# Seven products instead of eight in the down projection of a SwiGLU layer, on eight cores

## The chip, the cores and the metric

One Trainium2 chip, one launch on its 8 cores, 4 on each die. Each core computes a quarter of one sequence (2048 of the 16384 tokens) through the whole two-layer network; the cores do not exchange data. The metric is the device time of the slowest core in microseconds (us). A kernel has a fast state and, in some executions, a slow one, in which the cores of one die show a lower granted clock.

Names used below: PE is the matmul engine, DVE the vector engine, ACT the scalar engine, POOL the GpSimd engine. PSUM is the memory that PE writes its products to; the kernel uses eight banks of it (`ps0` to `ps7`), and a bank stays taken until its result has been read. A slab is a piece of a weight matrix that one transfer brings in. A "call" is one pass of the feed-forward layer (FFN) over half of a core's tokens, two tiles of 512. There are four: call 1 and 2 in layer 0 (first and second half of the tokens), call 3 and 4 in layer 1. "First-half calls" are 1 and 3, "second-half calls" 2 and 4. After call 2 the mixer and the attention of layer 1 follow; after call 4 the final norm and the store.

## The reference, cut to what matters

```python
D_MODEL, BATCH, SEQ, DEPTH = 1024, 2, 8192, 2
D_FF = 2816                                  # 22 chunks of 128

def swiglu(n, w_gate, w_up, w_down):
    return (jax.nn.silu(n @ w_gate) * (n @ w_up)) @ w_down

# in each of the two layers:
#   h = h + mixer(rms_norm(h))               (convolution in layer 0, gated MLP in layer 1)
#   h = h + cross_attention(rms_norm(h), memory)
#   h = h + swiglu(rms_norm(h, g_ffn[i]), ffn_w_gate[i], ffn_w_up[i], ffn_w_down[i])
# return rms_norm(h, g_final)
```

## The kernel before

The code is cut and shortened. Gate and up already use seven products for eight (Winograd's form of Strassen's scheme). A unit covers two hidden chunks of 128 for two token tiles: the weights are a 2 x 2 of blocks (2 chunks by 2 halves of the 1024 inputs), the tokens a 2 x 2 too (2 tiles by 2 halves). Each "p" below is a group of four matmuls of 512 columns; `g` is 0 for gate and 1 for up.

```python
FPARTS = (12, 10)                     # hidden chunks in each part
AHEAD = {"pe": 6, "act": 32, "dve": 32, "pool": 1, "sp": 1}     # window of the list scheduler
SWITCH = 4.0                          # its penalty for an ACT function of another table

# ffn_pair(): raw = weight block, sm = weight sum (sw), B11.. = tokens nT, T1, T2, T4 = token differences tw
def p1(g):                            # Z = A11 B11, copied to W
    mm(Z[g], raw(g, 0, 0), B11, False)
    act(self.ps[W[g]], self.ps[Z[g]])
def p5(g): mm(R[g], sm(g, 0), T1, False)
def p6(g):
    mm(Z[g], sm(g, 1), T2, True)      # onto Z
    act(V[g], self.ps[Z[g]])          # snapshot of the running sum
def p2(g): mm(W[g], raw(g, 0, 1), B21, True)    # + silu (g=0), product into hid (g=1)
def p7(g):
    mm(Z[g], raw(g, 1, 0), T3, True)  # snapshot Y, then DVE: Y = R + Y ...
def p4(g): mm(Z[g], raw(g, 1, 1), T4, True)
def p3(g): mm(R[g], sm(g, 2), B22, True)        # DVE: V = R + V ...
steps = ((p1,0),(p1,1),(p5,0),(p5,1),(p6,0),(p6,1),(p2,0),(p7,0),(p7,1),(p2,1),(p4,0),(p4,1),(p3,0),(p3,1))

# ffn(l, h): each part is gate and up, then a plain down projection of that part
for part, nf in enumerate(FPARTS):
    for i in range(nf // 2):
        ...                                        # weight sums one unit ahead, on DVE
        self.ffn_pair(*slabs[i], tts, i, npair + i, later)
    if part == 1 and h == 0:
        self.token_sums((2, 3))                    # differences of the next half's tokens
    if final and h == 1 and part == 1:
        self.last_down(l, tts, nf)                 # last tile in two halves of 256 columns
        continue
    for m in range(KC):
        w = self.wc(f"fd{part}", l, m)
        for ti, tt in enumerate(tts):
            ...   # linear(): nf matmuls; DVE: hT += ps; in the last part also the square for the next norm

# schedule(): of the ready instructions in an engine's window the one with the smallest
# due time (worked back from the end) goes first
o = min((o for o in go if o.ready <= t + self.SLIP),
        key=lambda o: (o.due + (self.SWITCH if o.table not in (None, table) else 0.0), o.n))
```

The softmax here doesn't subtract the row's maximum and nothing guards it: scores larger than these inputs give would overflow.

## Time and profile before

Median 1645.21 us of 6 runs (1641.37 to 1799.38). The stages of the program, read off PE's timeline as the distance between the first matmuls of consecutive stages, agree to 0.2 us in the FFN on all cores (but for call 1 on core 3, 210.8 us) and vary by several us in the rest:

| stage before | us |
|---|---|
| start to the first FFN call | 446 to 454 |
| call 1 / 2 / 3 | 209.7 / 210.3 / 209.7 |
| mixer and attention of layer 1, between call 2 and 3 | 332 to 337.5 |
| call 4 up to the mark | 197.8 |
| tail: from the mark to the end | 23.1 |

The mark is PE's first down matmul after the two 512-wide matmuls that sum the first tile's squares for the final norm (1619.3 us on the profiled core). PE's timeline shows rows of 256-wide matmuls from there on, and the expectations below call it the first half-wide matmul; but the first 256-wide matmul comes 4.8 us earlier (1614.5), inside a merged row. The prediction counts its tail, 27.9 us, from that one.

### The profile page before, as it was taken

To read this page: it belongs to the slowest core of one execution; us is meant where nothing else is said; L and a number is where in the kernel's file an instruction comes from. 1 tells how busy PE (TensorE), PEld (TensorE's weight loads), DVE (VectorE), ACT (ScalarE), POOL (GpSimd) and SP (SyncE) were. 2 spreads that over 40 slices of the span, in tenths; PEclk is the share of its full clock that TensorE was granted. 3 is DMA by queue.
4 is the path that set the end of the run, shared out by engine and by line. 5 is a ranking of instruction groups with operands and counts; after the bars stand their busy time and mean duration, and the time that the engine had idled before them with its cause. 6 is when DMAs were issued, how large, how long until landed. Compare 5 with 4: busy or idle time off the path is not lost.

```text
span 1642.4 us, 24105 instructions; the slowest of 8 cores (1629.0 to 1642.4 us)
## 1 busy us (share of the span) xinstructions
PE 1588.2 (97%) x7920; PEld 762.9 (46%) x7920; DVE 1025.9 (62%) x1662; ACT 712.3 (43%) x1176; POOL 71.3 (4%) x149
## 2 busy tenths in 40 slices
PE   5899899999999999999999999999999999999998
PEld 2344484444444444444443455544444444444445
DVE  3638856656787367683654864664689447685466
ACT  2622366455464053650435533455555134372243
POOL 1000000000000000000000000000000000000000
PEclk9899999999999999999999999999999999999999
DMA  8352248420235255443544134150043436375452
GB/s 183 120 104 40 39 77 199 101 50 1 47 60 100 51 94 100 78 87 68 94 80 78 30 74 78 26 91 1 1 77 71 84 69 124 65 153 120 74 90 104
DMA packets 34265, 130.66 MB, mean 80 GB/s; under 512 B 3680, under 2 KB 12256, under 8 KB 27616
## 3 DMA queue, kind: packets, MB, share of 16 engines
q0 software_dynamic: 18720, 100.03, 34.3%
q1 hardware_dynamic: 15424, 29.08, 5.9%
q8 instruction: 67, 1.10, 0.3%
q14 instruction: 54, 0.44, 0.1%
HBM read 216.51 MB, written 8.39 MB: 137 GB/s over the span
## 4 chain that ended last, share of the span: by engine, by line
PE 90%; DMA 4%; DVE 2%; issue 2%; ACT 1%; SPq 0%; DVEq 0%; POOL 0%; ACTq 0%; POOLq 0%
PE ps L619 63%; PE ps L617 23%; PE ps L110 2%; DMA hT<-x_in 1%; PE ps L1097 1%; PE ps L766 1%; DMA wbuf<-w_ev_in 1%; DVE t L110 1%; DMA wbuf<-w_od_v 1%; ACT t L110 1%; DVE wd L110 1%; DMA wbuf<-w_xqT 0%; PE ps L1042 0%; DMA yA<-yst 0%; DMA wbuf<-w_od_out 0%
## 5 line engine op out<-in xcount | busy, mean ns | idle before, releaser
L110 DVE TENSOR_TENSOR hT<-hT,ps 128x512 f32<-128x512 f32 (+1 forms) x264 | 176.9, 670 | 218.6 <-PE ps L619 214.8
L619 PE MATMUL ps<-hid,wbuf 128*128 128x512 f16 (+1 forms) x1488 | 306.4, 368 | 0.0
L619 PE MATMUL ps<-nT,wbuf 128*128 128x512 f16 x1216 | 277.7, 380 | 0.3 <-DVE nT L110 0.3
L619 PEld LDWEIGHTS ps<-hid,wbuf 128*128 128x128 f16 x1488 | 145.6, 98 | 158.9
L619 PEld LDWEIGHTS ps<-nT,wbuf 128*128 128x128 f16 x1216 | 117.8, 98 | 136.5 <-issue 2.1
L110 ACT ACTIVATE t<-ps 128x512 f32<-128x512 f32 (+1 forms) x192 | 111.0, 580 | 132.1 <-PE ps L619 87.0
L110 DVE TENSOR_TENSOR w<-ps,w 128x512 f32<-128x512 f32 x176 | 120.2, 690 | 75.0 <-PE ps L617 38.3
L617 PE MATMUL ps<-nT,wbuf 128*128 128x512 f16 x704 | 159.4, 379 | 0.6 <-ACT w L110 0.6
L110 ACT ACTIVATE w<-ps 128x512 f32<-128x512 f32 x176 | 104.6, 598 | 103.3 <-PE ps L617 102.8
L110 DVE SCALAR_TENSOR_TENSOR nT<-hT,vec,rs 128x512 f16<-128x512 f32 x192 | 135.7, 745 | 15.1 <-ACT rs L110 12.3
L110 ACT ACTIVATE ps<-ps 128x512 f32<-128x512 f32 x88 | 50.9, 582 | 204.1 <-PE ps L619 203.5
L619 PE MATMUL ps<-pT,VW 128*128 128x512 f16 x512 | 118.7, 379 | 2.9 <-DVE pT L110 2.9
L619 PE MATMUL ps<-nT,G 128*128 128x512 f16 x512 | 120.6, 379 | 0.0
L617 PEld LDWEIGHTS ps<-nT,wbuf 128*128 128x128 f16 x704 | 68.7, 98 | 84.2 <-issue 1.5
L110 ACT ACTIVATE sq<-hT 128x512 f32<-128x512 f32 x90 | 56.5, 629 | 105.7 <-DVE hT L110 99.5
L110 ACT ACTIVATE sqp<-hT 128x512 bf16<-128x512 f32 (+1 forms) x96 | 56.5, 594 | 101.0 <-DVE hT L110 40.7
L110 ACT ACTIVATE w<-w 128x512 f32<-128x512 f32 x88 | 55.5, 631 | 75.9 <-DVE w L110 73.2
L617 PE MATMUL ps<-nT,sw 128*128 128x512 f16 x352 | 83.8, 379 | 0.0
L617 PE MATMUL ps<-tw,wbuf 128*128 128x512 f16 x352 | 83.6, 379 | 0.1
L617 PE MATMUL ps<-tw,sw 128*128 128x512 f16 x352 | 83.5, 379 | 0.0
L619 PE MATMUL ps<-tw,sw 128*128 128x512 f16 x352 | 83.3, 379 | 0.0
L110 ACT ACT_TABLE_LOAD x52 | 66.7, 1283 | 32.0 <-DVE small L110 10.5
(112 smaller groups left out, 1771.6 us busy)
## 6 DMA issues: line engine op xcount, KB each, us to landing
wbuf<-w_fgu POOLq DMA_DIRECT2D x44, 1024.0 KB, 8.7
hT<-x_in SPq DMA_DIRECT2D x28, 512.0 KB, 8.1
wbuf<-w_fd POOLq DMA_DIRECT2D x16, 768.0 KB, 7.1
wbuf<-w_fd POOLq DMA_DIRECT2D x16, 640.0 KB, 6.2
out<-hT SPq DMA_DIRECT2D x12, 512.0 KB, 4.7
wbuf<-w_ev_in POOLq DMA_DIRECT2D x10, 512.0 KB, 7.8
wbuf<-w_xk POOLq DMA_DIRECT2D x8, 512.0 KB, 7.2
wbuf<-w_xv POOLq DMA_DIRECT2D x8, 512.0 KB, 7.8
```

The lines of the kernel that those rows point to most:

```text
L110: o = self.add(eng, lambda e: getattr(e, meth)(**kw), reads, writes, cost=_op_cost(eng, kw))
L617: ins = e.matmul(out, lhsT=l, rhs=r, start=False, stop=(i == np_ - 1), skip_group_check=True)
L619: ins = e.matmul(out, lhsT=l, rhs=r, start=(i == 0), stop=(i == np_ - 1))
L766: ins = e.matmul(self.ps[b][:, i * NMEM:(i + 1) * NMEM], lhsT=ws[i][0](k), rhs=mn[:, k, :], start=(k == 0), stop=(k == KC - 1))
L1097: ins = e.matmul(self.ps[b][:, i * NMEM:(i + 1) * NMEM], lhsT=w(c), rhs=self.kT[:, c, :], start=(hc == 0), stop=(hc == 1))
```

## The change

Its intent: the down projection too by seven products, so that PE has an eighth less of it to do. For that the hidden width is cut 8, 8, 6, each part gets two down units of 14 product groups, differences of hidden tiles (`ht`) and sums of down weights are formed, and the results are added to hT one by one. A helper, `tens`, is meant to let POOL take a share of the sums, but its first line sets DVE. The very last down projection (part 3 of call 4) stays plain. The diff, cut:

```diff
-FPARTS = (12, 10)
+FPARTS = (8, 8, 6)
-    AHEAD = {"pe": 6, "act": 32, "dve": 32, "pool": 1, "sp": 1}
+    AHEAD = {"pe": 6, "act": 32, "dve": 32, "pool": 40, "sp": 1}
-           ("fgu", 2, D, 2 * DFF), ("fd0", 2, FPARTS[0] * 128, D), ("fd1", 2, FPARTS[1] * 128, D)]
-WCOLS = {"fgu": 512, "od_v": 512, "xo": 512}
+           ("fgu", 2, D, 2 * DFF)] + [(f"fd{i}", 2, n * 128, D) for i, n in enumerate(FPARTS)]
+WCOLS = {"fgu": 512, "od_v": 512, "xo": 512, "fd0": 512, "fd1": 512, "fd2": 512}
+        self.ht, self.ht_s = self.tiles("ht", [128, 3, FMAX // 2, TT], FP16, 3 * FMAX // 2)
...
+    def tens(self, eng, dst, dst_s, i0, s0, i1, s1, op):
+        eng = "dve"
+        self.P.op(eng, "tensor_tensor", [s0, s1], [dst_s], out=dst, in0=i0, in1=i1, op=op)
...
+        end = ((p4, 0), (p3, 0), (p3, 1), (p4, 1)) if u.last else ((p4, 0), (p4, 1), (p3, 0), (p3, 1))
...   # gate_unit, after its products:
+            kb.tens(eng, *t(0), *dst(1, ia), *dst(0, ia), sub)
+            kb.tens(eng, *t(1), *dst(1, ib), *t(0), sub)
+            kb.tens(eng, *dst(1, ia), *dst(1, ib), *dst(1, ia), sub)
+            kb.tens(eng, *t(2), *dst(0, ib), *t(1), sub)
...   # down_unit: the seven products of hid and ht, and where their results go
+        def snap_add(ti, m, z, done):
+            v = kb.snap(z)                       # ACT copy of the running sum
+            add("pool", ti, m, v.t[:, :], v.slot, done)
+        u.r5 = lambda g, r: add("dve", 1, m0(g) + 1, *bank(r), False)
+        u.u2 = lambda g, z: snap_add(1, m0(g), z, False)
+        u.c11 = lambda g, w: add("dve", 0, m0(g), *bank(w), True)
+        u.u3 = lambda g, z, r: snap_add(1, m0(g) + 1, z, True)
+        u.c21 = lambda g, z: add("dve", 0, m0(g) + 1, *bank(z), True)
+        u.c12 = lambda g, r: add("dve", 1, m0(g), *bank(r), True)
...   # ffn(): one list of units, gate units of a part, then its two down units
+            plain = final and h == 1 and part == np_ - 1
+            for q in range(0 if plain else 2):
+                todo.append((f"fd{part}", 4 * q, self.down_unit(...), part, False))
```

Left out: POOL's cost in the scheduler, its DMA issues kept in order, and a slot that keeps the memsets of the setup in order.

## The prediction

> **What bounds the kernel now.** I read the page's first part and its chain of waits, then the costliest groups, then cut the feed-forward (FFN) stages out with the view of busy time by stretch, and went through the timeline of the vector engine (DVE) at a boundary of those stages and at the end of the kernel.
>
> From the page, engines, chain and groups:
> ```profile
> PE 1588.2 (97%) x7920; PEld 762.9 (46%) x7920; DVE 1025.9 (62%) x1662; ACT 712.3 (43%) x1176; POOL 71.3 (4%) x149
> ...
> PE 90%; DMA 4%; DVE 2%; issue 2%; ACT 1%; SPq 0%; DVEq 0%; POOL 0%; ACTq 0%; POOLq 0%
> ...
> L110 DVE TENSOR_TENSOR hT<-hT,ps 128x512 f32<-128x512 f32 (+1 forms) x264 | 176.9, 670 | 218.6 <-PE ps L619 214.8
> L619 PE MATMUL ps<-hid,wbuf 128*128 128x512 f16 (+1 forms) x1488 | 306.4, 368 | 0.0
> ```
> PE is the bound: 97% busy and 90% of the chain. The down projection is the group that reads hid, 1488 matmuls that never wait (last column 0.0). Its results are added to hT by DVE, which mostly waits for PE (218.6 us idle): there DVE has room.
>
> Busy time in the four FFN calls (two layers, two halves of the tokens; the fourth without its last down projection). Columns: stretch, length, PE, weight loads, DVE, ACT, POOL, PE clock, DMA:
> ```profile
> 454.35:664.06 209.71, 209.68 (x971) 94.73 (x970) 137.62 (x223) 81.71 (x134) 9.49 (x18) 1.00 0.42 78
> 664.06:874.30 210.24, 209.93 (x973) 95.05 (x972) 124.61 (x189) 85.85 (x136) 10.02 (x19) 1.00 0.44 82
> 1211.80:1421.50 209.70, 209.67 (x971) 94.74 (x970) 137.79 (x223) 81.57 (x134) 9.49 (x18) 1.00 0.43 78
> 1421.50:1597.20 175.70, 175.39 (x813) 79.39 (x812) 106.24 (x161) 77.85 (x122) 8.97 (x17) 1.00 0.55 108
> ```
> PE has no hole in 800 us at full clock, so here a matmul removed is time removed, unless something new makes PE wait. DVE is busy 66, 59, 66 and 60%. What it has left is the budget of this change.
>
> The chain in order of time gives the pitch of a matmul:
> ```profile
> 598.45 3.62 PE L617 MATMUL ps<-nT,wbuf 128*128 128x512 f16 x16
> 601.90 1.89 PE L617 MATMUL ps<-tw,wbuf 128*128 128x512 f16 x8
> 603.63 1.89 PE L617 MATMUL ps<-nT,sw 128*128 128x512 f16 x8
> 605.35 1.89 PE L619 MATMUL ps<-nT,wbuf 128*128 128x512 f16 x8
> ```
> (This is PE's timeline.) Sixteen matmuls take 601.90 - 598.45 = 3.45 us and eight take 1.725, so 0.2158 us each. The 379 ns of the groups are durations that overlap.
>
> DVE's timeline in a gate unit:
> ```profile
> 512.82 0.68 DVE L110 TENSOR_TENSOR hid<-ps,t 128x512 f16<-128x512 f32 x1
> 513.41 0.68 DVE L110 TENSOR_TENSOR hid<-w,w 128x512 f16<-128x512 f32 x1
> 514.18 0.69 DVE L110 TENSOR_TENSOR hid<-ps,t 128x512 f16<-128x512 f32 x1
> 514.97 0.69 DVE L110 TENSOR_TENSOR w<-ps,w 128x512 f32<-128x512 f32 x1
> ```
> A 512-wide instruction lasts 0.69, but the next can start 0.60 later. Over the first FFN call the mean is 137.62/223 = 0.617 us. I use 0.62 for these and for the 1024-wide fp16 weight sums, and 0.37 for 512-wide fp16 (the group of tw has 32 in 11.7 us, 419 ns each).
>
> **What the Trainium skill says.** "VectorE: DVE Perf Modes", section on the TRN2 errata, gives (N+151)/0.96 ns for an fp32 tensor_tensor, 691 ns at 512; the trace has 686 to 690. The same page's perf-mode tier table lets tensor_tensor run at twice the rate in 16 bits from SBUF and not with PSUM; 419 ns for 512 and 690 for 1024 fp16 elements agree. "TensorE: Matmul & The Clock Gate", Back-to-back issue gap, has N/2.4+2.5, about 216 ns, for the isolated gap and about 131 ns for a sustained stream; the trace's stream has 215.8, so it contradicts the second. "Perfetto Trace Analysis", Optimizing Scalar/DVE Operations, says that the write-acknowledgement half of the access overhead overlaps with the next instruction; starts 0.60 apart at 0.69 duration agree in direction.
>
> **The change part by part.** The gate and up projections already use the seven-product scheme (Winograd's form of Strassen's). The change extends it to the down projection: the hidden width is split 8, 8, 6 instead of 12, 10, each part gets two down units of 14 product groups in place of 16, and combinations of hidden tiles (ht) and of down weights (sw) have to be formed. The helper that should choose between POOL and DVE sets DVE on its first line: all new sums are DVE work, POOL gets none.
>
> PE. A full call had 22 x 8 x 2 = 352 down matmuls and gets 7/8, 308: 44 less. The fourth call keeps its last six chunks plain: 16 x 8 x 2 = 256 become 224, 32 less. 3 x 44 + 32 = 164, times 0.2158 = 35.4 us, or 2.15% of 1645. This is the ceiling: other stages don't change.
>
> DVE, full call. PSUM additions go from 32 to 48 (4 per column pair, 2 pairs, 2 units, 3 parts): 16 more. Snapshots added from SBUF: 24. Down weight sums: 4 x 6 = 24, of which 8 are 768 wide (0.49 estimated). Sums of hidden tiles: 4 x 11 = 44 in fp16. 56 x 0.62 + 8 x 0.49 + 44 x 0.37 = 34.7 + 3.9 + 16.3 = 55 us. The call shrinks by 9.5 us to 200. So DVE needs 137.6 + 55 = 193 of 200 us (96%) in both calls of the first half and 180 of 201 (90%) in the second layer-0 call; the fourth gets (16 + 16 + 16) x 0.62 + 32 x 0.37 = 42. In all DVE goes from 1026 to about 1230.
>
> By unit: a gate unit is 56 matmuls, 12.08 us, with 12 x 0.62 + 4 x 0.37 = 8.9 of DVE. A down unit with four chunks also has 12.08 us and 16 x 0.62 = 9.9. A down unit of the last part has 42 matmuls, 9.06 us, and 12 x 0.62 + about 2 = 9.4, already more than PE. Into these two (18.1 us) the first half also has to fit the 16 token differences of the next half (16 x 0.37 = 5.9), some 7 us more than fits; squares for the norm (12 x 0.62) can wait. Banks hold about four groups of lag, 3.4 us, and the next gate unit needs little DVE at first. I put PE's wait from saturation at 4 us per first-half call: 8 us.
>
> ACT: 24 snapshots and 12 PSUM copies at 0.60 are 22 us per call on 82 of 200: no bound.
>
> Hand-over from gate to down. After the last gate unit the fifth product needs hidden difference T1. From the end of the third last group DVE has the addition, product and difference: 0.4 wait, 0.69, 0.1, 0.69, 0.1, 0.42, about 2.4 us; PE has three groups of 0.86 = 2.6 to hide it, which is why the change moves those groups. With a foreign instruction between them it is missed by about 0.5 us. Eleven hand-overs: 5.5 us.
>
> Tail. From 1614.5 to 1642.4 the last tile ran 27.9 us, 17.3 of it from matmuls that will need about 11. But the first tile's scaling started only 8.8 us after that point (1623.29), and 8 x 0.66 + 16 x 0.4 of DVE scaling still follows. I estimate 24.5, so 3.6 us of the 7 are not realised.
>
> DMA. Slabs become uniform, the ring holds three of 8 KB per partition; a slab is asked for about 14 us before its first sum and lands in 8.7. Hidden. PE's wait of 4.0 us for w_od_v becomes about 1.3 shorter, since the last weights come free earlier.
>
> Sum: -35.4 + 8 + 5.5 + 3.6 - 1.3 = -19.6, so 1626.
>
> **The rivals.** (a) DVE keeps up. For it: static order by due time, a cautious cost of 0.69 each, room in the banks. Then only tail and od_v remain: -33, 1612, at the edge of 2%. Against it: 96% in the first halves. (b) DVE becomes the bound in all FFN stages, because it takes instructions in fixed order and loses 10% to its own waits for ACT, PE and weights: first halves need 212 us against 209.7 before, second ones 198; with the tail the result lies near 1640 to 1650. For it: the dependent starts in the timeline lie 0.79 apart, not 0.60. Against it: with a backlog other work fills those gaps. (c) The weights come late after the narrow units: a first-in-order wait of DVE of 2 us per half, 8 us more, 1634. The 8.7 us landing and 14 us lead speak against it.
>
> **Range and chances.** The ceiling of 35.4 leaves only 2.5 us of loss for over 2% faster (below 1612), and the tail alone may take that: 0.12. Losing over 68 us would need DVE to fail far beyond (b): 0.06. Eight in ten: 1612 to 1646.
>
> **What would show it.** Right: PE matmuls near 7756, hid without plain groups but in the last call, DVE near 1230 us and 95% in the first-half calls, PE's waits led by DVE ht and by banks that DVE frees, most at the ends of the first halves. Wrong: DVE idle there while PE is full (rival a), PE idle steadily within gate units (b), DVE waits on w_fgu or w_fd before waits of PE (c), or a lower clock in fast runs.

## More of the kernel before

The prediction shows the engines, the chain and the FFN calls. One view more is needed later: the groups of DVE in call 1, with different shapes kept apart. Columns: names and shapes, count, then busy time and mean ns, then idle time just before them and its releasers.

```profile
L110 DVE TENSOR_TENSOR hT<-hT,ps 128x512 f32<-128x512 f32 x32 | 22.0, 686 | 31.4 <-PE ps L619 31.3
...
L110 DVE TENSOR_TENSOR sqa<-sqa,sq 128x512 f32<-128x512 f32 x12 | 8.2, 689 | 5.4 <-ACT sq L110 5.2 <-DVE sqa L110 0.2
...
L110 DVE TENSOR_TENSOR tw<-nT,tw 128x512 f16<-128x512 f16 x12 | 4.4, 421 | 0.3 <-PE ps L617 0.3
```

In call 1 before the change DVE is idle for 31.4 us just ahead of its additions to hT, waiting for PE, and the sums of squares (sqa) and the next half's token differences (tw) are all made inside the call.

## The result and the profile after

The output is correct. After: median 1623.37 us of 7 runs (1623.15 to 1691.21, one of them slow); before, on the same chip: median 1643.88 of 16 (1641.29 to 1856.59). The ratio of the fast runs is 0.9882 (95% interval 0.9871 to 0.9893). Ratios here are the mean time of one kernel's fast runs over that of the other's in the same rounds, so not quite the ratio of the two medians. It is 1.2% faster: within the 2% that count as the same, and 2.6 us below the predicted 1626.

The page, engines and chain:

```profile
PE 1552.6 (96%) x7724; PEld 739.7 (46%) x7724; DVE 1224.3 (76%) x2066; ACT 781.0 (48%) x1304; POOL 67.1 (4%) x141
...
PE 86%; DMA 5%; DVE 5%; issue 2%; ACT 1%; SPq 0%; DVEq 0%; POOL 0%; ACTq 0%; POOLq 0%
```

PE's busy time fell by 35.6 us, the predicted ceiling (35.4), but the span fell by only 22.9 in these two profiles; DVE's share of the chain went from 2 to 5%. PE still sets the end, and it now waits.

Busy time in the stretches that answer to those of before: calls 1, 2, 3, call 4 up to its plain down projection, and the rest. Columns: stretch, length, PE, weight loads, DVE, ACT, POOL, PE clock, DMA.

```profile
452.04:653.55 201.51, 200.83 (x928) 90.06 (x927) 176.94 (x301) 95.03 (x157) 8.33 (x16) 1.00 0.44 77
653.55:857.32 203.77, 201.68 (x929) 89.94 (x928) 179.60 (x309) 107.50 (x176) 9.55 (x19) 1.00 0.52 90
1194.82:1396.53 201.71, 200.82 (x927) 90.05 (x926) 176.92 (x301) 95.02 (x157) 8.32 (x16) 1.00 0.42 76
1396.53:1584.55 188.02, 183.40 (x845) 81.86 (x844) 161.65 (x273) 96.72 (x158) 8.05 (x16) 1.00 0.54 110
1584.55:1619.50 34.95, 24.30 (x162) 15.74 (x162) 27.21 (x55) 15.06 (x31) 0.00 (x0) 0.89 0.35 121
```

The stages as in the table of before. The ceiling is the number of removed 512-wide matmuls times 0.2158 us: 44 in each full call. In call 4 the 32 removed are put down to the tail: because the plain part is 4 chunks shorter, as many matmuls as before the change (888) run ahead of the first 256-wide one, and 64 of 256 columns fewer after it. By the mark this is off by 0.2 us. Counted from the first 256-wide matmul itself, call 4 goes from 193.0 to 198.4 us and the tail from 27.9 to 24.7, which says the same.

| stage | before | after | change | ceiling | not realised |
|---|---|---|---|---|---|
| call 1 | 209.7 | 201.5 | -8.2 | -9.5 | 1.3 |
| call 2 | 210.3 | 203.8 | -6.5 | -9.5 | 3.0 |
| call 3 | 209.7 | 201.7 | -8.0 | -9.5 | 1.5 |
| call 4, up to the mark | 197.8 | 203.4 | +5.6 | 0 | 5.6 |
| tail | 23.1 | 19.8 | -3.3 | -6.9 | 3.6 |
| sum | | | -20.4 | -35.4 | 15.0 |

Start, mixer and attention: 450.2 and 334.7 before, 449.0 and 334.9 after, means of eight cores that differ from one another by several us. Nothing is claimed from those.

The total agrees with the prediction, but the losses do not lie where it put them: the first-half calls lose 2.8 us together, the second-half ones 8.6. PE's waits in call 2 (first fence) and in call 4 (second); columns: what waited and for whom, us in total, times, longest:

```profile
PE ps L624 <- DVE ht L110: 0.9, 1, 0.9
PE ps L624 <- DVE hid L110: 0.6, 1, 0.6
PE ps L622 <- DVE hid L110: 0.3, 1, 0.3
```

```profile
PE ps L624 <- DVE hid L110: 1.9, 2, 1.0
PE ps L624 <- DVE ht L110: 1.8, 1, 1.8
PE ps L622 <- DVE hid L110: 0.5, 1, 0.5
```

Few waits. The 0.6 in call 2 and one of the two for hid in the first line of call 4 (0.9) are for a bank of PSUM inside a gate unit, the other of these two (1.0) is at the start of the plain part, and the rest are at hand-overs from the gate units of a part to its down units. The longest, in call 4 on the profiled core, can be followed through three engines' timelines. ACT, DVE and PE from 1446 to 1454 us (start, duration, what, count, and in brackets the idle time before and the releaser):

```profile
1446.47 1.28 ACT L110 ACT_TABLE_LOAD   x1
1447.77 0.63 ACT L110 ACTIVATE rs<-t 128x512 f32<-128x512 f32 x1
1448.57 0.58 ACT L110 ACTIVATE ps<-ps 128x512 f32<-128x512 f32 x1 [0.18 <-PE ps L624]
1449.17 1.28 ACT L110 ACT_TABLE_LOAD   x1
1450.47 0.63 ACT L110 ACTIVATE w<-w 128x512 f32<-128x512 f32 x1
```

```profile
1451.27 0.69 DVE L110 TENSOR_TENSOR hid<-w,w 128x512 f16<-128x512 f32 x1 [0.71 <-ACT w L110]
1452.07 0.42 DVE L110 TENSOR_TENSOR ht<-hid,hid 128x512 f16<-128x512 f16 x1
```

```profile
1449.81 1.02 PE L622 MATMUL ps<-hid,wbuf 128*128 128x512 f16 x4 [0.52 <-DVE hid L110]
1452.64 1.89 PE L624 MATMUL ps<-ht,sw 128*128 128x512 f16 x8 [1.81 <-DVE ht L110]
```

The last silu of the gate unit (w<-w) is held up by two loads of ACT's function tables: one for the exponential of the first half's norm (rs<-t), one to go back to silu. DVE's product of hidden chunks waits for it, the difference ht follows, and PE stands for 1.81 us. DVE had stood idle for 0.71 us just ahead of that product, so here it was ACT that held up the chain, and not a backlog of DVE.

On some cores such a wait costs more than itself. The same place on core 3: PE's timeline, then the stretch that follows the wait (columns as in the table of stretches above):

```profile
1441.83 3.39 PE L624 MATMUL ps<-ht,sw 128*128 128x512 f16 x8 [1.81 <-DVE ht L110]
```

```profile
1441.80:1445.20 3.40, 3.37 (x9) 1.26 (x10) 3.40 (x10) 0.00 (x0) 0.00 (x0) 0.54 0.79 161
```

The eight matmuls after the wait take 3.39 us there against 1.89 on the profiled core, at a granted clock of 0.54. Cores 3 and 5 take 1.5 and 1.7 us more for call 4 than the other six, which waited as long. The medians of eight cores used below leave this out unless more than half of the cores have it.

Why the norm of the first half runs there is seen in DVE's groups of call 1, the same view as above:

```profile
L110 DVE TENSOR_TENSOR hT<-hT,ps 128x512 f32<-128x512 f32 x47 | 31.7, 685 | 6.5 <-PE ps L622 4.6 <-PE ps L624 1.5
...
L110 DVE TENSOR_TENSOR hT<-hT,w 128x512 f32<-128x512 f32 x18 | 11.6, 684 | 0.0
...
L110 DVE TENSOR_TENSOR sqa<-sqa,sq 128x512 f32<-128x512 f32 x4 | 2.7, 686 | 0.2 <-DVE sqa L110 0.2
L110 DVE TENSOR_TENSOR tw<-nT,tw 128x512 f16<-128x512 f16 x6 | 2.2, 418 | 0.0
```

The idle time ahead of the additions to hT is spent (31.4 to 6.5 us). Of 12 sums of squares only 4 are left in the call, of 24 additions of snapshots (hT<-hT,w) 18, of 12 token differences of this form 6. The rest ran later: call 2 has 27 of those additions. The scheduler moved what no matmul needed at once; of this only the token differences (0.3 to 6.3 us after the start of call 2) are needed by PE soon after.

There the moved work is met again 25 us after the start of call 2. DVE (first fence) and PE (second):

```profile
677.27 0.69 DVE L110 TENSOR_TENSOR sqa<-sqa,sq 128x512 f32<-128x512 f32 x1
678.14 0.69 DVE L110 TENSOR_TENSOR sqp<-sqa,sq 128x512 bf16<-128x512 f32 x1 [0.17 <-ACT sq L110]
678.75 0.68 DVE L110 TENSOR_TENSOR sw<-wbuf 128x1024 f16<-128x1024 f16 x1
679.35 1.28 DVE L110 TENSOR_TENSOR hid<-ps,t 128x512 f16<-128x512 f32 x2
```

```profile
680.18 1.89 PE L624 MATMUL ps<-tw,sw 128*128 128x512 f16 x8 [0.57 <-DVE hid L110]
```

The products of hidden chunks, which set two banks of PSUM free, stand behind squares of the first half, and PE waits for a bank. The same place in call 4 costs 0.93. Counting the distances between the starts of PE's groups less 0.2158 us for each matmul, call 4 on the profiled core has five gaps that make up most of its 5.6 us: 1.1 for this bank, 0.7 and 2.0 at the first hand-over, 0.2 at the second and 1.2 at the first matmul of the plain part, and a few of 0.1.

### The profile page after: what moved, and what is told of

Same layout as the page of the kernel before. It is cut to its first block, busy times and chain, and to the rows that moved or that the text cites. A ratio compares the mean times of both kernels' runs of the same rounds, so it can differ in the third digit from the quotient of the medians.

```text
span 1619.5 us, 24981 instructions; the slowest of 8 cores (1608.0 to 1619.5 us)
## 1 busy us (share of the span) xinstructions
PE 1552.6 (96%) x7724; PEld 739.7 (46%) x7724; DVE 1224.3 (76%) x2066; ACT 781.0 (48%) x1304; POOL 67.1 (4%) x141
## 3 DMA queue, kind: packets, MB, share of 16 engines
q0 software_dynamic: 17568, 100.03, 35.6%
## 4 chain that ended last, share of the span: by engine, by line
PE 86%; DMA 5%; DVE 5%; issue 2%; ACT 1%; SPq 0%; DVEq 0%; POOL 0%; ACTq 0%; POOLq 0%
PE ps L624 49%; PE ps L622 33%; DMA hT<-x_in 2%; PE ps L110 2%; DMA wbuf<-w_xqT 1%; DVE hT L110 1%; PE ps L1102 1%; PE ps L771 1%; DMA wbuf<-w_ev_in 1%; DVE t L110 1%; DMA wbuf<-w_od_v 1%; DVE hid L110 1%; DVE wd L110 1%; PE ps L1047 0%; ACT t L110 0%
## 5 line engine op out<-in xcount | busy, mean ns | idle before, releaser
L110 DVE TENSOR_TENSOR hT<-hT,ps 128x512 f32<-128x512 f32 (+1 forms) x328 | 217.7, 672 | 116.7 <-PE ps L624 91.8
L110 ACT ACTIVATE w<-ps 128x512 f32<-128x512 f32 x264 | 156.5, 598 | 181.4 <-PE ps L622 169.6
L110 DVE TENSOR_TENSOR w<-ps,w 128x512 f32<-128x512 f32 x176 | 120.4, 690 | 32.7 <-ACT w L110 16.4
L110 ACT ACTIVATE ps<-ps 128x512 f32<-128x512 f32 x132 | 76.7, 582 | 126.3 <-PE ps L624 111.2
L624 PEld LDWEIGHTS ps<-pT,VW 128*128 128x128 f16 x512 | 50.0, 98 | 63.7 <-issue 3.8
L624 PEld LDWEIGHTS ps<-nT,G 128*128 128x128 f16 x512 | 50.1, 98 | 60.4
L622 PE MATMUL ps<-hid,wbuf 128*128 128x512 f16 x328 | 75.2, 379 | 2.2 <-DVE hid L110 1.6
```

What stands on the lines that cost most here:

```text
L110: o = self.add(eng, lambda e: getattr(e, meth)(**kw), reads, writes, cost=_op_cost(eng, kw))
L622: ins = e.matmul(out, lhsT=l, rhs=r, start=False, stop=(i == np_ - 1), skip_group_check=True)
L624: ins = e.matmul(out, lhsT=l, rhs=r, start=(i == 0), stop=(i == np_ - 1))
```

## The experiments

Twelve kernels ran. All figures of stages are medians of the eight cores; the last two columns are the time and the ratio to the kernel before.

| kernel | call 1 | call 2 | call 3 | call 4 | tail | us | ratio (95%) |
|---|---|---|---|---|---|---|---|
| after | 201.5 | 203.8 | 201.7 | 203.4 | 19.8 | 1623.4 | 0.9882 (0.9871 to 0.9893) |
| e1_pool_as_written | 215.3 | 215.0 | 214.6 | 212.3 | 20.4 | 1668.5 (lowest) | 1.0166 (1.0134 to 1.0198) |
| e2_parts_only | 210.1 | 212.1 | 210.1 | 205.8 | 19.7 | 1652.3 | 1.0048 (1.0032 to 1.0064) |
| e3_no_last_ht (wrong output) | 200.2 | 202.4 | 200.2 | 201.2 | 19.7 | 1616.5 | 0.9827 (0.9809 to 0.9844) |
| e4_more_dve | 201.5 | 220.2 | 201.5 | 213.9 | 19.8 | 1658.2 | 1.0080 (1.0062 to 1.0098) |
| e5_no_reorder | 201.6 | 204.1 | 201.6 | 201.7 | 19.7 | 1621.1 (lowest) | 0.9863 (0.9842 to 0.9885) |
| e6b_no_table (wrong output) | 201.5 | 202.7 | 201.7 | 200.3 | 19.7 | 1620.4 | 0.9857 (0.9837 to 0.9876) |
| e7_no_scale (wrong output) | 201.5 | 203.8 | 201.7 | 203.4 | 19.6 | 1624.4 | 0.9879 (0.9861 to 0.9896) |
| e8_tail_pool | 201.5 | 203.8 | 201.7 | 203.4 | 21.3 | 1625.2 | 0.9887 (0.9868 to 0.9907) |
| e9_head | 202.8 | 203.8 | 202.5 | 206.0 | 19.7 | 1627.6 | 0.9903 (0.9887 to 0.9919) |
| e10_switch | 201.5 | 204.4 | 201.5 | 201.4 | 19.6 | 1620.9 | 0.9866 (0.9847 to 0.9885) |
| e11_686 | 201.6 | 202.6 | 201.5 | 201.1 | 21.0 | 1625.2 | 0.9866 (0.9842 to 0.9889) |
| e12_688 | 201.5 | 207.2 | 201.5 | 200.2 | 21.0 | 1625.2 | 0.9880 (0.9862 to 0.9899) |

Differences of 0.3% between ratios are within their intervals. The stages decide more sharply: in each call of the kernel after, at least six of the eight cores agree to 0.1 us. (Call 4 is given up to the mark.) The kernels ran in several sessions and on more than one chip, each time beside the kernel before, whose median there lay between 1643.6 and 1644.8.

The first theory was the prediction's own: DVE is full at the end of first-half calls, and PE waits for it there. Its rival: DVE never stops PE by being full, and what is lost comes from single waits at the hand-overs and at the tail.

**e1_pool_as_written.** Let POOL take the sums that the code names for it.

```diff
-        eng = "dve"
```

> The helper's override is taken away, so the sums that the change asks of POOL (products, hidden differences of all but the last gate unit of a part, additions of snapshots) run there. If DVE's load is what costs the changed kernel, DVE falls by about 90 to 110 us and the time falls by some 5 to 10 us (1613 to 1618). If POOL is slow (over 1 us for a 512-wide instruction), or blocks behind its own transfers, or slows DVE, PE gets new waits and the time rises above 1630. I think the second likelier.

Correct, and slower than the kernel before: 1.0166. Every call takes 9 to 14 us longer than in the kernel after. (The boundaries of all calls can be read on cores 0 and 3; the table has their means.) POOL's and DVE's groups, shapes kept apart, and PE's longest wait, on its profiled core:

```profile
L110 POOL TENSOR_TENSOR hT<-hT,w 128x512 f32<-128x512 f32 x88 | 130.3, 1505 | 99.4 <-ACT w L110 99.3
L110 POOL TENSOR_TENSOR hid<-w,w 128x512 f16<-128x512 f32 x64 | 90.0, 1406 | 187.9 <-DVE w L110 96.7 <-ACT w L110 62.8 <-PE ps L622 20.3
```

```profile
L110 DVE TENSOR_TENSOR hT<-hT,ps 128x512 f32<-128x512 f32 x312 | 209.4, 682 | 110.0 <-PE ps L624 102.0 <-PE ps L622 5.4
...
L110 DVE TENSOR_TENSOR sw<-sw,wbuf 128x1024 f16<-128x1024 f16 x60 | 78.5, 1309 | 9.1 <-PE ps L622 8.8 <-DVE sw L110 0.3
```

```profile
PE ps L622 <- DVE w L110: 32.6, 14, 3.8
```

POOL took 272 instructions from DVE (2066 became 1794), worth about 140 us by the prediction's rates (152 at 0.62 and 120 at 0.37), and DVE's busy time fell only from 1224 to 1217 us: what it kept got slower. One of the four kinds of weight sums, all with both inputs in SBUF, went from 689 to 1309 ns (the other three, 687 to 689 before, to 715, 874 and 1125), while the additions with one input in PSUM stayed at 682. The Trainium skill, "SBUF — State Buffer", section "Who interferes with whom", says just this: a DVE instruction with two SBUF inputs contends with a POOL instruction that reads SBUF, one with a single SBUF input, outside the modes that use two ports for one input, does not. So the override in `tens` is worth some 47 us (the difference of the two ratios times 1644): without it the change would have lost.

**e2_parts_only.** The kernel before with the parts 8, 8, 6, 512-wide down slabs and the smaller weight ring of the change, down projection still plain.

```diff
-FPARTS = (12, 10)
+FPARTS = (8, 8, 6)
-WCOLS = {"fgu": 512, "od_v": 512, "xo": 512}
+WCOLS = {"fgu": 512, "od_v": 512, "xo": 512, "fd0": 512, "fd1": 512, "fd2": 512}
-        self.off = sw_lo - 2 * FMAX * TT * 2
+        self.off = sw_lo - 2 * FMAX * TT * 2 - 3 * FMAX * TT      # room of ht, left empty
```

> The kernel before with the hidden width in parts of 8, 8, 6, 512-wide down slabs and the smaller weight ring, but plain down products. If those parts of the change are free, the time stays within 3 us of before (1641 to 1647), PE has 7920 matmuls and the last tile's share behaves as in the changed kernel: the stage from the first half-wide matmul to the end near 20 us rather than 23. If the ring or the third part costs, it is 5 us or more above that.

Correct; 7.5 us slower than the kernel before. Its tail is 19.7, as after the change: with six chunks in the last part the 256-wide matmuls take 6.9 us less, but the tail gets only 3.4 shorter. So what the tail does not give back belongs to the split, not to the seven products. In call 2 PE has one wait that the kernel before has not:

```profile
PE ps L619 <- DVE hid L110: 1.6, 1, 1.6
```

So a part of call 2's loss (1.8 us against the kernel before) also comes from the split alone, without any difference ht. The wait is at the first hand-over, 51 us after the start of the call: two table loads of ACT (at 46.4 and 48.4 us) stand just ahead of the last silus of the gate unit, as in call 4 of the change; whether they cause this wait was not tested. Seven products then take 28.9 us off this kernel in medians of different rounds (1652.3 to 1623.4), 27 by the two ratios.

**e3_no_last_ht.** What do the hand-overs cost? The down units read the differences of the next to last chunk in place of the last one's, so that PE need not wait for the last gate unit's. The output is wrong.

```diff
-            u.B[nm] = ([ht[:, j, k, :] for k in range(n)], ts[j * (FMAX // 2):j * (FMAX // 2) + n])
+            u.B[nm] = ([ht[:, j, min(k, n - 2), :] for k in range(n)], ts[j * (FMAX // 2):j * (FMAX // 2) + n - 1])
```

> The changed kernel with a result that is wrong on purpose: in the down units the last chunk reads the hidden differences of the chunk before it, so no down product waits for the last gate unit's sums in ht; all work is still done. If the hand-over from gate to down costs what I predicted, 0.5 us at each of 11, the time falls by about 5 us. From the waits seen in the changed kernel's trace (0.1 us at most hand-overs, 0.9 and 1.8 at the first of the second halves) I now expect 3 to 4 us less (1619 to 1621), nearly all in the second-half calls. If these waits only move to the next product, nothing changes.

Calls 1 and 3 come to 200.2 us each, which is 209.7 - 9.5: exactly the ceiling. In a first-half call the hand-over is the whole loss; nothing besides is lost to a full DVE. Over the four calls it takes 1.3 + 1.4 + 1.5 + 2.2 = 6.4 us, 0.58 for each of eleven hand-overs. What remains is 1.6 us in call 2, 3.4 in call 4 and the tail. In this kernel's profile the wait for the bank is 1.4 us in call 2 (0.7 in the change: half of what call 2's hand-over gave back is waited for here) and 1.0 in call 4, the start of the plain part 1.2, and the first hand-over of call 4 still 0.7, for a hidden chunk and not a difference: 4.3 of those 5.0, by the same count of gaps.

**e4_more_dve.** Is DVE full? The last difference of each gate unit is computed five times: 44 instructions and some 16 us more of DVE in each full call.

```diff
-            kb.tens(eng, *t(2), *dst(0, ib), *t(1), sub)
+            for _ in range(5):
+                kb.tens(eng, *t(2), *dst(0, ib), *t(1), sub)
```

> The changed kernel with the last of the four hidden differences of each gate unit computed five times (same values): 4 x 0.37 = 1.5 us of DVE per gate unit, 16 us per full call, 60 in all. If DVE is at its bound in these calls, as I predicted for the first halves, PE waits for most of it and the time rises by 20 us or more. If DVE still has slack of some 20 us per call, as its 177 of 201 busy us say, the time rises by less than 8, mostly at the start of the second-half calls.

Correct; 33 to 35 us slower than the kernel after (by the ratios and by the medians). The first-half calls stay at 201.5 us. Call 2 grows by 16.4, call 4 by 10.5, the mixer and attention between calls 2 and 3 by 8.6 on average. Calls 1 and 2 (columns as above), and a wait of PE over the whole execution:

```profile
454.60:656.10 201.50, 200.82 (x928) 90.12 (x927) 176.77 (x323) 94.61 (x157) 8.35 (x16) 1.00 0.42 76
656.10:876.30 220.20, 205.28 (x930) 90.21 (x929) 198.37 (x365) 105.55 (x174) 11.17 (x22) 0.98 0.45 84
```

```profile
PE ps L622 <- DVE tw L110: 10.3, 4, 4.6
```

DVE is busy for 177 us of call 1 here as in the kernel after, although it was given 16 us more to do: the surplus leaves the call. It piles up behind the boundary, where the token differences of the next half (tw) are needed at once and are late. So there is a bound, which this kernel passes: DVE's backlog goes from a first-half call to a second-half one, and as long as the token differences come in time it costs nothing at the end of the first. How far the kernel after is from the bound was not measured. Some 2 to 3 of the 16.4 us are matmuls at about half the clock after the long waits, on every core.

**e5_no_reorder.** The reordered last four groups of the last gate unit of a part, put back.

```diff
-        end = ((p4, 0), (p3, 0), (p3, 1), (p4, 1)) if u.last else ((p4, 0), (p4, 1), (p3, 0), (p3, 1))
+        end = ((p4, 0), (p4, 1), (p3, 0), (p3, 1))
```

> The changed kernel without its reordering of the last four product groups in the last gate unit of each part. If the chain addition, product, difference after the last of them sets the start of the down units, it now starts 0.86 us later at each of ten or eleven hand-overs: 6 to 9 us more (1629 to 1632), the first half going from 201.5 to about 204. If the other wait, for the second row of hid, was what held PE, the time stays within 2 us.

A miss. Four of its six runs were slow; the two fast ones took 1621.06 and 1622.05 us, and the calls are 201.6, 204.1, 201.6 and 201.7: no worse than with the reordering, and 1.7 better in call 4. PE's timeline at the first hand-over of call 1, with the reordering (first fence) and without it (second):

```profile
498.58 1.89 PE L622 MATMUL ps<-nT,sw 128*128 128x512 f16 x8
500.31 1.03 PE L622 MATMUL ps<-tw,wbuf 128*128 128x512 f16 x4
501.17 1.89 PE L624 MATMUL ps<-hid,wbuf 128*128 128x512 f16 x8
503.15 1.89 PE L624 MATMUL ps<-ht,sw 128*128 128x512 f16 x8
```

```profile
501.74 1.89 PE L622 MATMUL ps<-nT,sw 128*128 128x512 f16 x8
503.47 1.89 PE L624 MATMUL ps<-hid,wbuf 128*128 128x512 f16 x8
505.32 1.02 PE L622 MATMUL ps<-hid,wbuf 128*128 128x512 f16 x4
506.18 1.89 PE L624 MATMUL ps<-ht,sw 128*128 128x512 f16 x8
```

The last four groups did run in the old order; but then the scheduler by itself put one more group of the down unit, which needs hidden chunks and no difference, ahead of the first that reads ht. The chain is hidden either way. And in call 4 the reordering costs: it makes the fourth product the last, whose hidden chunk the plain part needs at once. The wait at the start of the plain part (1.2 us in the change) is gone here.

**e6_no_table** and **e6b_no_table.** Second theory: the long waits at the first hand-over of second-half calls are due to table loads for the first half's norm. The logarithm and the exponential of that norm are replaced by copies, which need no other table. In the second the norm's factor is a constant 0.5. Wrong output.

```diff
     def rstd_bc(self, src_s, src, n, scale, ec, plain=False):
+        if plain:
+            r = self.rsr.next()
+            self.act(t.t[:, 0:n], t.slot, src, src_s)
+            P.op("act", "activation", [t.slot], [r.slot], out=r.t[:, 0:n], in_=t.t[:, 0:n], func=AF.Copy,
+                 scale=0.0, bias=0.5)
+            return r
-        jobs = [self.main_job(tt, gcol, final) for tt in tts]
+        jobs = [self.main_job(tt, gcol, final, plain=h == 0) for tt in tts]
```

> The changed kernel with a result that is wrong on purpose: the norms at the end of the first-half calls take Copy in place of Ln and Exp, so ACT has the same instructions but no change of its table in the second-half calls. If these loads (1.28 us each, one of them right in the chain of the first hand-over of the last call) are a cause of the second-half losses, layer 0's second call falls from 203.8 by 1 to 2 us, the last from 203.4 by 2 to 3, 3 to 5 us in all (1618 to 1620). If DVE's backlog alone is the cause, under 1 us.

> As e6_no_table, which the check refused for a value that overflowed; now the two Copies give a constant, so the result is wrong on purpose and finite. ACT has the same instructions but no table change for the first-half norms. If table loads are a cause of the second-half losses: layer 0's second call from 203.8 to about 202.3, the last (up to the last tile) from 203.4 to about 200.5 to 201.5, 3 to 5 us in all. If not: under 1 us, as taking away the scalings did.

Table loads fell from 48 to 36. Call 2 gets 1.1 us faster, call 4 3.1, calls 1 and 3 stay. PE's long waits for ht at the first hand-over of the second-half calls are gone. So the loads of this norm cost 4.2 us. Most of it is not besides the 6.4 of the hand-overs but within it: a wait that a load lengthens counts in both, and of the 6.4, 3.6 lie in the second-half calls.

The loads as such are not new. The kernel before has 6 in call 2 and 8 in call 4, the kernel after 6 and 6. But before, those for the first half's norm lie 17 to 38 us after the start of call 4, and the first matmul of down comes 74 us after it; after the change they lie at 36 to 53 us, because the squares come later, and the first hand-over at 51 to 56, because the first part has 8 chunks instead of 12. Both moved toward each other.

**e7_no_scale.** Rival to that: not the loads, but DVE's backlog from the first half is in the way at the hand-over. In call 4 the sixteen scalings of the first half's final output are left out (wrong output), some 10 us of DVE.

```diff
-            j.scale(k)
-            j.scale(k + 1)
+            if tt > 1:
+                j.scale(k)
+                j.scale(k + 1)
```

> The changed kernel with a result that is wrong on purpose: the first half's output of the last layer is stored without its 16 scalings, 10.6 us less for DVE early in the last call. If DVE's backlog costs the last call its extra time, that call falls from 203.4 by 2 us or more, the rest staying as it is. If the table loads and the hand-over are the causes, it falls by less than 1.

No change in call 4 (203.4 us on most cores). But this run says little about the rival: in the kernel after those scalings lie 96 to 177 us after the start of call 4, behind the first hand-over (51 to 56), so that they could not be in its way. What speaks against the rival is DVE's idle time of 0.71 us just ahead of the product that the hand-over waits for (0.72 in call 2), and e6b. The squares, which also come over from the first half, were not taken away alone; that they hold up the bank is read from the timeline, not shown by a run.

**e8_tail_pool.** The tail: DVE has no hole in its last 13 us, shown here for the kernel after, and the last lines are the scalings of the final norm.

```profile
1604.52 4.72 DVE L110 SCALAR_TENSOR_TENSOR hT<-hT,vec,rs 128x512 f32<-128x512 f32 x7
1609.16 1.40 DVE L110 TENSOR_TENSOR hT<-hT,ps 128x256 f32<-128x256 f32 x4
1610.48 6.41 DVE L110 SCALAR_TENSOR_TENSOR hT<-hT,vec,rs 128x256 f32<-128x256 f32 x16
```

So two of the eight rows of each piece went to POOL (times the norm's factor) and ACT (times the gain).

```diff
+            if pool:
+                (gcol, dst_k, dst_s), = scales
+                P.op("pool", "tensor_tensor", [src_s[k], r.slot], [src_s[k]], out=src_k(k), in0=src_k(k),
+                     in1=r.t[:, 0:n], op=ALU.mult)
+                P.op("act", "activation", [src_s[k], self.vec_s], [dst_s[k]], out=dst_k(k), in_=src_k(k),
+                     func=AF.Copy, scale=self.vcol(gcol + k))
+                return
```

> The changed kernel, correct, with the scalings of two of the eight rows in the last call's three final pieces taken from DVE: POOL multiplies by the reciprocal root (1.5 us a full-width row in e1), ACT by the gain. DVE is busy without a hole in the last 13 us; 2.9 us less of it make the tail 17 to 18 us instead of 19.6 if it is the bound and POOL doesn't slow it; near 19.6 or more if POOL's port use stretches the other scalings, as e1 showed for two-input instructions (689 to 1309 ns).

A miss: the tail got 1.5 us longer (21.3 against 19.8). POOL took 2.94 us for two 512-wide products, and the first of DVE's scalings, started with POOL running, took 1.86 us in place of 0.75:

```profile
1604.61 1.86 DVE L110 SCALAR_TENSOR_TENSOR hT<-hT,vec,rs 128x512 f32<-128x512 f32 x1 [0.17 <-ACT rs L110]
```

The same conflict as in e1, on single instructions: the last six 256-wide scalings, again beside POOL, took 3.49 us, where sixteen took 6.41 in the kernel after.

**e9_head.** Another way at the hand-over: in the first down unit of a part the second product, which needs hidden chunks and no difference, comes before the fifth.

```diff
+        if u.head:
+            steps = ((p1,0),(p1,1),(p2,0),(p2,1),(p5,0),(p5,1),(p6,0),(p6,1),(p7,0),(p7,1)) + end
+            later = {{5: 6, 6: 8, 8: 9}.get(k, k): v for k, v in later.items()}
```

> The changed kernel, correct, with another order in the first down unit of each part: the second product (which needs only hid and the copy in W) comes before the fifth, so the differences in ht have 1.7 us more. If the hand-over's wait for ht is what the run with the last chunk taken away removed (about 6.4 us), most of it goes: 1617 to 1619. Against it stands the wait for ACT's copy into W, about 0.1 us at each; if that takes its place, the gain is under 2 us.

A miss: calls 1 and 3 lose about 1 us, call 4 loses 2.6, of which 1.6 is the lower clock after a long wait: five of the eight cores have it, and the other three lose 1.0. In call 4 the wait for ht is still there (2.2 us on the profiled core), and waits for ACT's copy W, which the second product goes onto, appear.

**e10_switch.** The scheduler's penalty for an ACT function of another table from 4 to 16, so that it would group them.

```diff
-    SWITCH = 4.0
+    SWITCH = 16.0
```

> The changed kernel, correct, with the scheduler's charge for changing ACT's table raised from 4 to 16, so that it groups Ln and Exp. If table loads in the hand-over are a cause, there are fewer than 48 of them and the second-half calls lose 1 to 3 us; if the grouped work comes later and holds up norms elsewhere (cross-attention, the second mixer), the time rises by up to 5.

Correct. 42 loads in place of 48; call 4 is 201.4 on every core (2.0 faster), call 2 is 204.4 (0.6 slower). 1620.9 us is the lowest median of the kernels with a correct output, but its interval (0.9847 to 0.9885) overlaps that of the change (0.9871 to 0.9893): that it is faster is shown for call 4, not for the whole.

**e11_686** and **e12_688.** With that penalty, the order of the parts: the plain part with 8 chunks, the short one second or first.

```diff
-FPARTS = (8, 8, 6)
+FPARTS = (8, 6, 8)      # e11;  (6, 8, 8) in e12
-    SWITCH = 4.0
+    SWITCH = 16.0
```

> The table-switch penalty of e10 (16) and the hidden parts in the order 8, 6, 8: the short part is in the middle, and the last, plain part of the last call has 8 chunks again. The three full calls make the same products, so they should stay at 201.5, 204 and 201.7 us. In the last call the plain part saves 28 instead of 32 matmuls of down (0.9 us worse), but two more chunks of plain matmuls, 8 x 2 x 2 x 0.1079 = 3.5 us, move behind the first half-wide matmul, so that the stage ahead of it gets shorter by about 2.6 us (from e10's 201.4 to 198 to 199) and the tail longer by up to 3.5 us in matmul time. Theory A: the 19.8 us tail with 6 chunks is bound by VectorE, which has no hole in it, so the extra matmuls lie beside work that VectorE does anyway, the tail goes to about 21 and the sum is 1 to 3 us below e10: 1618 to 1620. Theory B: the tail is matmul bound in its first part, it goes to 23.1 as before the change, and the sum is 0 to 1 us above e10: 1621 to 1622.

> As e11 but with the parts in the order 6, 8, 8: the short part comes first, so that the first hand-over of a call comes earlier, after 6 chunks of gate and up rather than 8. If it is the backlog of VectorE (deferred squares and scalings of the first half) at the start of a second-half call that hurts the first hand-over, there is less time to work it off, and the second-half call gets slower than in e11 by 0.5 to 2 us, last call too: 1620 to 1623. If the hand-over is independent of the backlog, e12 is the same as e11 within 0.5 us.

In e11 the tail is 21.0, as theory A had it: of the 3.5 us of matmuls that moved behind the boundary 1.4 show. But call 4 is not the 198 to 199 us expected: on four cores it takes 199.2 to 200.1, which with the tail is within 0.8 us of e10, and on the other four 202.2 to 204.3, for which the theory had no term. On the profiled core DVE and then PE show why:

```profile
1556.02 0.69 DVE L110 TENSOR_TENSOR sw<-wbuf 128x1024 f16<-128x1024 f16 x1 [5.88 <-DMA wbuf<-w_fgu]
```

```profile
1557.46 3.01 PE L622 MATMUL ps<-nT,sw 128*128 128x512 f16 x8 [3.47 <-DVE w L110]
```

The weight sum stood first in DVE's fixed order, its slab had not landed, and everything behind it waited. It is rival (c) of the prediction, in another kernel. The first half's output was being stored in the same stretch; that the store delays the slab was not tested. In e12 call 2 is 4.6 us longer than in e11, the direction expected of an earlier first hand-over and more than its 0.5 to 2 us; on the three cores without the lower clock it is 3.0 longer. Call 4 takes 200.1 to 200.4, no less and up to 1.2 us more than on those cores of e11 whose slab came in time. (e10's 201.4 is no measure: with its plain part of 6 chunks some 12 matmuls more, about 2.5 us, lie ahead of the mark.) So an earlier first hand-over costs time in call 2 and little in call 4. Whether it is by DVE's backlog is not shown: on core 1, in call 2, two table loads again stand ahead of the silu that the first hand-over waits for, and DVE is idle for 0.62 us before it. Neither beats e10, so no version here is shown to beat the change by more than the spread of the times.

## Why the prediction was right, step by step, and where it was not

- **PE ceiling, 35.4 us: right.** PE's busy time fell by 35.6. The count "near 7756" was wrong: it took 7920 less 164 full-width matmuls, while the trace counts instructions, and in call 4 the plain part's second tile has two of 256 columns for each of 512. So 3 x 44 + 64 = 196 fewer, 7724, as the page has it.
- **DVE's added work: right in sum, wrong in place.** 1224 us against 1230 predicted. A first-half call has 177 where 193 was predicted; the missing 16 us are squares, additions of snapshots and token differences that ran after the call. The second-half call of layer 0 has the predicted 180, but by luck: it took in this work and passed some of its own on to the mixer.
- **Saturation, 8 us in the first-half calls: the step that failed.** "I put PE's wait from saturation at 4 us per first-half call." The runs show 0 there besides the hand-over: without it a first-half call is exactly at its ceiling (e3), and with 16 us more of DVE it is unchanged (e4). The prediction had said that squares can wait, but let the surplus cost time at the end of the same call instead of following it into the next one. There, beyond the hand-over, 1.6 and 3.4 us are lost, 5.0 together. Of these 2.4 are waits for a bank that stands behind moved squares, and 1.2 are at the start of the plain part, which come from the reordering (e5) and not from a full DVE. So the step was put in the wrong calls and was too large: 8 us, where at most 5.0 and by the traces some 2.4 are lost.
- **Hand-over, 5.5 us: nearly right.** 6.4 (e3). Its reason is only half of it: without the reordering that was to hide the chain the scheduler hides it as well (e5), and the longest waits are those where table loads fall into the chain (e6b), which the prediction did not name.
- **Tail, 3.6 us not realised: right.** By the prediction's own count, from the first 256-wide matmul, 24.5 us were predicted and 24.7 measured (27.9 before); by the mark 3.6 of 6.9 us are not realised. It goes with the split of the parts (e2), and DVE's scalings fill its end.
- **w_od_v, -1.3: the wait, not the time.** The wait went from 4.0 to 2.5 us, but the stage that holds it is as long as before (334.7 and 334.9 on average). It should not have been in the sum.
- **Rivals.** (a) holds for the first-half calls, (b) for none of the calls of the change; in e4, with more work for DVE, PE does wait for it. (c) did not occur in the change; it did in e11.

Together, 8 + 5.5 + 3.6 - 1.3 = 15.8 predicted and 6.4 + 5.0 + 3.6 = 15.0 measured. The sum was closer than its parts, and that is luck: the term for saturation was too large and in the wrong place, and losses that the prediction did not name (the start of the plain part, the table loads) filled it.

Left open: some 0.7 of the 5.0 us are not traced to a wait, and the part of the squares in it was not tested by a run of its own. The changed order of POOL's setup work was not tested alone either, and the stages outside the FFN vary by several us from core to core, in which a small effect of it would not be seen. Why the clock falls on some cores after a wait and not on others is not known.

## What to carry to other kernels

When an engine has more to do than a stage holds, ask where the scheduler puts the surplus before charging it to that stage: work that nothing needs soon moves on and meets something else later, here a chain from gate to down that had not been there. Read the engines' timelines of the kernel before for rare events (table loads, stores) near the places where the change will create a dependency. And do not hand DVE's two-input SBUF work to POOL without a run: the instructions that stay behind may pay for it.

## What the Trainium skill lacked or had wrong

- "TensorE: Matmul & The Clock Gate", Back-to-back issue gap: about 131 ns for a sustained stream of 512-wide matmuls; a stream of sixteen in a row runs at 215.8 ns each here, and the 164 that were removed took 35.6 us of PE's busy time with them, 217 ns each. What the page calls the isolated gap is right for the stream.
- "ScalarE: Activation LUTs", What ACT_TABLE_LOAD costs: 1283 ns for the load agrees (1283 here), but the 1380 ns of drain that it adds to every switch do not show: a copy started at 1448.57 for 0.58 us, the load started at 1449.17 and the next ACTIVATE at 1450.47, 1.30 us later.
- "GPSIMD Engine Reference", 3.1 Elementwise: 4497 ns for a two-input add of 2048 elements in fp32; a quarter of it, 1124 ns as an estimate for 512, is short of the 1406 to 1505 ns in e1 for fp32 inputs, and two of them took 2.94 us in e8. But the quarter leaves out any fixed part, and here POOL ran beside DVE: that the page's figure is wrong is not shown.
- "SBUF — State Buffer", Who interferes with whom, is right and has no size for a kernel's mean: 689 became 1309 ns for one kind of fp16 weight sums and 874 and 1125 for two others, 745 became 837 for scalings with two SBUF inputs, over a whole execution with POOL busy 28% of the time.
